# A two-layer hybrid encoder on one core: the last layer's residual in two exact parts, two tiles' statistics on ScalarE, and the order of two matmuls in the mean square

## The chip, the cores and the metric

The kernel runs on one core of one Trainium2 chip. The metric is the device time of the whole kernel in microseconds (us): the median over runs. A core has TensorE (PE in the profile, with its weight loads shown as PEld), VectorE (DVE), ScalarE (ACT), GpSimd (POOL) and SyncE (SP, which only issues DMAs here). Each engine takes its own instructions strictly in the order in which they are written into its queue, and waits at an instruction until what it reads is there and what it overwrites is no longer needed.

## The reference, cut to what matters

Two layers on a 1024 x 1024 fp32 input. Layer 0 has dilated attention and a gated linear attention (GLA), layer 1 a gated scan with 12 heads (HGRN2). Each layer ends in an output projection, a residual and a layer norm:

```python
def _layer_norm(z, g, b):
    mu = jnp.mean(z32, axis=-1, keepdims=True)
    var = jnp.mean(jnp.square(z32 - mu), axis=-1, keepdims=True)
    out = (z32 - mu) * lax.rsqrt(var + NORM_EPS) * g + b

def _head_rmsnorm(o, gain):
    o = o * lax.rsqrt(jnp.mean(o * o, axis=-1, keepdims=True) + NORM_EPS)
    return o.reshape(o.shape[0], o.shape[1], -1) * gain

# layer 1
q, f_f, f_b, i, gate = _split(proj, (C_WIDTH,) * 5)
o = bidirectional_gated_scan(qh, k_f, g_f, k_b, g_b, heads(i))
y = _head_rmsnorm(o, norm_gain) * jax.nn.silu(gate)
out = jnp.einsum('bsf,fd->bsd', y, w_out)
# every layer
x = _layer_norm(DEEPNORM_ALPHA * x + mixer(x), ln_gain[layer], ln_bias[layer])
```

## The kernel before, in words

**Exact parts.** The kernel keeps fp32 accuracy on TensorE by splitting an operand into a part rounded to fp32r (the H part, made by an ScalarE copy) and the exact rest (the L part, made by a subtraction on VectorE). A product is then three fp32r matmuls: H by H, L by H, H by L (`project`, lines 237 to 239; `out_units`; `final_units`, lines 321 to 323).

**Stages.** Attention runs first, then four GLA heads, then twelve HGRN heads. For every head 128 columns of the input projection are made in two halves of 512 tokens (hf 0 and 1) out of `xH[hf]` and `xL[hf]`, the transposed activations, which are 128 x 8 x 512 tiles that live through the layer. The head's scan has two directions d and two halves: `prep(d, hf)` makes decayed queries and keys, `keys` the states, `scores` the local products, `output(hf)` the head's result. The order within an HGRN head is (1,1), (1,0), (0,0), output(0), (0,1), output(1). In `prep`, VectorE scans the log gates (line 743), ScalarE takes exponentials (`gE`, `qi`, `ki`), GpSimd makes about ten small factors from `gE` (lines 763 to 781, from `eT` through `Gq`, `Gk`, `F3q`, `F3k` to `dec`), and VectorE multiplies them in (lines 756 to 799). The scores need `k2`, which needs `Gk`; the transposed keys need `k3`, which needs `F3k`. Before the gates of the last direction the head switches ScalarE's function table to the sigmoid and back (`sigmoids`); the second of the two sigmoids there needs the head's last projected block.

**Mean square.** `output` squares the head's result, splits the square into `sqH` (ScalarE, line 902) and `sqL` (VectorE, line 904), and sums it over partitions with two matmuls against a tile of ones, `sqH` first (lines 905 and 906). There are 8 such sums in the GLA stage and 24 in the HGRN stage.

**The end of the last layer.** Heads 10 and 11 leave their output projection to `final_units`. For each of the eight token tiles, `pre` puts the residual `z[i]` into two PSUM banks by an fp32 matmul against the identity (line 312), and `mul` adds twelve fp32r matmuls (lines 321 to 323). Tiles 4 to 7 are hf 1; tiles 4 and 6 use the two `pj` banks, tiles 5 and 7 the `s` and `o` banks, so tile 6 waits until tile 4 has been normalized. `layer_norm` takes the statistics on VectorE (line 374), and then, for tiles 0 to 5, normalizes on ScalarE (line 391), multiplies the gain on VectorE (line 392) and adds the bias on GpSimd (line 393); tiles 6 and 7 do all of that on VectorE (lines 382 and 384). The result goes out by DMA.

**Order.** A tile scheduler fixes each engine's order when the kernel is built, from the program's order, priorities and its own idea of when operands are ready. Work under `high_priority` is placed as if it stood 3000 instructions earlier.

Of the kernel before, what the change touches and what calls it, by code (L numbers as in the profile page):

```python
# [7 lines left out]
F32 = mybir.dt.float32  # L8
F32R = mybir.dt.float32r
U32 = mybir.dt.uint32  # L10
AF = mybir.ActivationFunctionType
ALU = mybir.AluOpType
# [3 lines left out]
P = 128  # L16
D = 1024
# [110 lines left out]
class Trunk:  # L128
# [156 lines left out]
    def final_units(self, w, f0, ys, norm, banks, reload):  # L285
# [7 lines left out]
        def weights(key):  # L293
# [12 lines left out]
                held[key] = first, res  # L306
            return held[key]

        def pre(hf, t):
            ps = [self.ps.tile([P, HALF], F32, tag=tag, name="fin", bufs=2) for tag in banks[hf][t % 2]]  # L310
            for c in range(2):
                mm(ps[c], self.ident, self.z[hf * 4 + t][:, c * HALF:(c + 1) * HALF], start=True, stop=False)
            tiles[hf, t] = ps

        def mul(hf, t):
            ts = slice(t * P, (t + 1) * P)
# [47 lines left out]
                res.append(t)  # L364
        return res

    def layer_norm(self, pool, i, params, direct=False, src=None):

        nc = self.nc
        zs = [self.z[i][:, c * HALF:(c + 1) * HALF] for c in range(2)]  # L370
        src = src or zs
        st = pool.tile([P, 2, 6], F32, tag="gt", name="st", bufs=2)
        for c in range(2):
            nc.vector.bn_stats(st[:, c, :], src[c])
        mv = pool.tile([P, 4], F32, tag="eT", name="mv", bufs=2)
        nc.vector.bn_aggr(mv[:, 0:2], st)
        mu, r, b = (mv[:, k:k + 1] for k in (0, 2, 3))
        self.act(r, mv[:, 1:2], AF.Ln, bias=self.epsz)
        self.act(r, r, AF.Exp, scale=-0.5)
        if direct:  # L380
            for c in range(2):
                nc.vector.scalar_tensor_tensor(zs[c], src[c], mu, params[c], op0=ALU.subtract, op1=ALU.mult)
            for c in range(2):
                nc.vector.scalar_tensor_tensor(zs[c], zs[c], r, params[2 + c], op0=ALU.mult, op1=ALU.add)
            return
        nc.vector.scalar_tensor_tensor(b, mu, -1.0, r, op0=ALU.mult, op1=ALU.mult)
        if src is zs:
            nc.scalar.activation(self.z[i], self.z[i], AF.Identity, scale=r, bias=b)
        for c in range(2):
            if src is not zs:  # L390
                nc.scalar.activation(zs[c], src[c], AF.Identity, scale=r, bias=b)
            nc.vector.tensor_tensor(zs[c], zs[c], params[c], op=ALU.mult)
            nc.gpsimd.tensor_tensor(zs[c], zs[c], params[2 + c], op=ALU.add)
# [300 lines left out]
class ScanHead(Item):  # L694
# [181 lines left out]
    def output(self, hf):  # L876
# [25 lines left out]
        nc.scalar.copy(sH, sq[0])  # L902
        sL = pool.tile([P, HALF], F32R, tag="k3", name="sqL", bufs=self.nbuf)
        nc.vector.tensor_tensor(sL, sq[0], sH.bitcast(F32), op=ALU.subtract)
        mm(ms, T.ones, sH, start=True, stop=False)
        mm(ms, T.ones, sL, start=False, stop=True)
        rs = pool.tile([P, HALF], F32, tag="tmp", name="rs", bufs=2)
        T.act(rs, ms, AF.Ln, scale=1.0 / self.V, bias=T.eps)
        T.act(rs, rs, AF.Exp, scale=-0.5)
# [222 lines left out]
def trunk_kernel(tc, x, x_t, w_in_ab, gla_gate_up, gla_gate_bias, gla_norm, w_out_ab, w_in_c, hgrn_lower_bounds,  # L1132
                 hgrn_norm, w_out_c, rel_bias, ln_gain, ln_bias, onehot, ident, mask, out):
    nc = tc.nc
    with ExitStack() as ctx:
# [14 lines left out]
        def scan_consts(pool):  # L1150

            T.restart = pool.tile([P, HALF], mybir.dt.uint8, tag="restart", name="restart")
            nc.gpsimd.memset(T.restart, 1)
            nc.gpsimd.memset(T.restart.rearrange("p (n c) -> p n c", c=16)[:, :, 0:1], 0)
            T.mask = pool.tile([P, P], U32, tag="mask", name="mask")
            nc.gpsimd.dma_start(T.mask, mask)
            T.ones = pool.tile([P, P], F32R, tag="ones", name="ones")
            nc.scalar.copy(T.ones, T.one.broadcast_to([P, P]))

# [90 lines left out]
        def ln1(i, halves):  # L1250
            if 1 not in lnp:
                lnp[1] = T.ln_params(hp, (("E", 5), ("E", 5)), ln_gain[1:2, :], ln_bias[1:2, :])
            T.layer_norm(hp, i, lnp[1], i in DIRECT[1], halves)
            if i in DIRECT[1]:
                for c in range(2):
                    nc.sync.dma_start(outv[:, i, c * HALF:(c + 1) * HALF], T.z[i][:, c * HALF:(c + 1) * HALF])
# [113 lines left out]
```

## Time and profile before

| what | value |
|---|---|
| time, median of 3 runs | 1990.66 us (1989.68 to 1991.99) |
| time of the profiled execution | 1991.2 us |
| its span (first to last instruction) | 1989.4 us |
| TensorE busy | 1914.5 us, 96% of the span |
| VectorE, ScalarE, GpSimd busy | 1320.6, 1010.1, 334.1 us |
| TensorE's mean granted clock | 0.992 of full speed |

The profile is of one execution; its time stands 0.5 us above the median. A span shown as x4 or x8 in the trace is a run of equal instructions. One fp32 matmul shows as two records of TensorE.

### The profile page before, as it was taken

What the parts mean: (1) busy time and instruction counts of PE and PEld (TensorE: products, weight loads), DVE (VectorE), ACT (ScalarE), POOL (GpSimd) and SP (SyncE); (2) the same over time, 40 slices, a digit from 0 to 9 for tenths busy, and PEclk for the clock granted to TensorE, in tenths of its full rate; (3) what the DMA queues carried; (4) which work ended last, traced back from release to release, by engine and by line L of the source; (5) the groups of instructions that cost most, each with busy time, mean ns of one, the idle gap of its engine ahead of it and who ended that gap; (6) DMA issues with size and microseconds to landing.
All of it is one profiled execution on the core that took longest, in us unless ns stands there. A gap on an engine that the chain in (4) does not pass through costs nothing.

```text
span 1989.4 us, 35447 instructions
## 1 busy us (share of the span) xinstructions
PE 1914.5 (96%) x13887; PEld 1571.8 (79%) x13887; DVE 1320.6 (66%) x2761; ACT 1010.1 (51%) x1847; POOL 334.1 (17%) x848
## 2 busy tenths in 40 slices
PE   7999999999999999999999999999999999999997
PEld 4777777787787878867878888888888888888875
DVE  4697878774776675677767646655764664676478
ACT  4666656553544343444556445535544642654473
POOL 1110202001211111111123112111311111131124
PEclk8999999999999999999999999999999999999999
DMA  8321212123111212112411211121121112112112
GB/s 234 71 50 33 50 38 45 31 77 95 43 50 50 64 53 70 53 43 69 124 43 43 64 54 44 38 80 33 33 79 49 33 48 71 32 39 89 40 44 85
DMA packets 142866, 118.59 MB, mean 60 GB/s; under 512 B 15301, under 2 KB 122565, under 8 KB 142699
## 3 DMA queue, kind: packets, MB, share of 16 engines
q1 hardware_dynamic: 130027, 102.55, 17.6%
q0 software_dynamic: 4512, 11.47, 2.4%
q10 hardware_dynamic: 8160, 2.31, 0.6%
q8 instruction: 109, 1.79, 0.4%
q14 instruction: 58, 0.48, 0.1%
HBM read 108.19 MB, written 8.11 MB: 58 GB/s over the span
## 4 chain that ended last, share of the span: by engine, by line
PE 46%; DVE 8%; ACT 4%; DMA 3%; issue 2%; POOL 1%; DVEq 0%; ACTq 0%; POOLq 0%
PE pj L237 9%; PE pj L238 9%; PE pj L239 9%; PE kv L818 3%; DVE g L743 2%; PE po L271 2%; PE po L272 2%; PE s L844 2%; PE po L273 2%; PE pj L249 1%; PE pj L250 1%; PE pj L251 1%; DMA wraw<-in_w_in_c_dram 1%; PE o L888 1%; PE o L892 1%
## 5 line engine op out<-in xcount | busy, mean ns | idle before, releaser
L237 PE MATMUL pj<-xH,wH 128*128 128x512 f32 x1280 | 512.7, 401 | 2.8 <-DVE kl L531 1.3
L238 PE MATMUL pj<-xL,wH 128*128 128x512 f32 x1280 | 508.1, 397 | 0.0
L239 PE MATMUL pj<-xH,wL 128*128 128x512 f32 x1280 | 507.4, 396 | 0.0
L199 ACT CAST wH<-wraw 128x512 fp32r<-128x512 f32 x248 | 153.5, 619 | 294.3 <-PE pj L238 180.3
L200 DVE TENSOR_TENSOR wL<-wraw,wH 128x512 fp32r<-128x512 f32 x248 | 170.8, 689 | 195.2 <-ACT wH L199 182.8
L237 PEld LDWEIGHTS pj<-xH,wH 128*128 128x128 f32 x1280 | 242.0, 189 | 51.1 <-issue 2.0
L239 PEld LDWEIGHTS pj<-xH,wL 128*128 128x128 f32 x1280 | 241.9, 189 | 46.3 <-issue 0.2
L238 PEld LDWEIGHTS pj<-xL,wH 128*128 128x128 f32 x1280 | 242.1, 189 | 44.2
L763 POOL TENSOR_TENSOR eT<-gE 128x16 f32<-128x16 f32 x64 | 30.2, 472 | 1038.2 <-ACT gE L158 1038.2
L249 PE MATMUL pj<-wH,xH 128*128 128x256 f32 x640 | 182.1, 285 | 0.4 <-ACT v L726 0.3
L250 PE MATMUL pj<-wL,xH 128*128 128x256 f32 x640 | 180.8, 283 | 0.0
L251 PE MATMUL pj<-wH,xL 128*128 128x256 f32 x640 | 180.7, 283 | 0.0
L276 DVE TENSOR_TENSOR z<-z,po 128x512 f32<-128x512 f32 x200 | 134.9, 682 | 63.5 <-PE po L273 62.7
L271 PE MATMUL po<-woH,yH 128*128 128x512 f32 x336 | 138.3, 421 | 9.7 <-ACT woH L217 6.3
L272 PE MATMUL po<-woL,yH 128*128 128x512 f32 x336 | 134.7, 401 | 0.7 <-DVE woL L218 0.6
L273 PE MATMUL po<-woH,yL 128*128 128x512 f32 x336 | 132.2, 394 | 0.0
L249 PEld LDWEIGHTS pj<-wH,xH 128*128 128x128 f32 x640 | 122.0, 191 | 4.3 <-ACT v L726 1.0
L250 PEld LDWEIGHTS pj<-wL,xH 128*128 128x128 f32 x640 | 122.1, 191 | 2.9
L251 PEld LDWEIGHTS pj<-wH,xL 128*128 128x128 f32 x640 | 122.0, 191 | 2.7
L271 PEld LDWEIGHTS po<-woH,yH 128*128 128x128 f32 x336 | 62.0, 188 | 33.9 <-ACT woH L217 10.9
L818 PE MATMUL kv<-v,k3T 128*128 128x128 f32 (+1 forms) x448 | 80.0, 313 | 7.9 <-DVE stb L830 5.2
L217 ACT CAST woH<-wraw 128x512 fp32r<-128x512 f32 x80 | 47.5, 616 | 76.9 <-PE po L273 26.7
(230 smaller groups left out, 3841.0 us busy)
## 6 DMA issues: line engine op xcount, KB each, us to landing
wraw<-in_w_in_c_dram SPq DMA_DIRECT2D x152, 256.0 KB
wraw<-in_w_in_ab_dram SPq DMA_DIRECT2D x96, 256.0 KB
wraw<-in_w_out_c_dram SPq DMA_DIRECT2D x44, 256.0 KB
wraw<-in_w_out_ab_dram SPq DMA_DIRECT2D x40, 256.0 KB
z<-in_x_dram SPq DMA_DIRECT2D x8, 512.0 KB
strip<-line POOLq DMA_DIRECT2D x8, 448.0 KB, 5.8
park<-sp SPq DMA_DIRECT2D x14, 256.0 KB
out_dram<-z SPq DMA_DIRECT2D x6, 512.0 KB
```

Source lines behind the costliest of these rows:

```text
L199: self.nc.scalar.copy(h, raw)
L200: self.nc.vector.tensor_tensor(lo, raw, h.bitcast(F32), op=ALU.subtract)
L237: mm(ps[:m], wH, xH[:, k, :], start=(k == 0), stop=False)
L238: mm(ps[:m], wH, xL[:, k, :], start=False, stop=False)
L239: self.lastmm = mm(ps[:m], wL, xH[:, k, :], start=False, stop=(k == last)).ins
L249: self.nc.tensor.matmul(o, xH, wH, start=(k == 0 and i % 2 == 0), stop=False)
L250: self.nc.tensor.matmul(o, xH, wL, start=False, stop=False)
L251: self.lastmm = self.nc.tensor.matmul(o, xL, wH, start=False, stop=(k == KT - 1 and i % 2 == 1)).ins
L271: mm(ps, yH[:, ts], h, start=(b == 0), stop=False)
L272: mm(ps, yH[:, ts], lo, start=False, stop=False)
L273: mm(ps, yL[:, ts], h, start=False, stop=(b == nb - 1))
L818: nc.tensor.matmul(kv[:, j, :], k3T[:, t, :], self.val(hf * 4 + t), start=True, stop=True)
```

## The change

1. In the last layer, for hf 1, the residual of tiles 4 to 7 is split ahead: ScalarE copies `z[4+t]` into two of the eight columns of `xH[0]` (rounded to fp32r), GpSimd subtracts that from `z` into `xL[0]`. Both tiles are dead once the last head's hf 0 projection has read them. `pre` then uses two fp32r matmuls against `identr`, an fp32r identity that ScalarE makes at the start of each of the two later stages, in place of one fp32 matmul. hf 0 keeps the fp32 matmuls.
2. Tiles 4 and 5 of the last layer take their statistics on ScalarE: a copy with a running sum and a square with a running sum for each 512 columns, with three one-column operations on VectorE between them, in place of two `bn_stats` and one `bn_aggr`.
3. In every mean square `sqL` enters the sum first and `sqH` second.

```diff
+        def split(t):
+            z = self.z[4 + t]
+            zH, zL = (x[0][:, 2 * t:2 * t + 2, :].rearrange("p a c -> p (a c)") for x in (self.xH, self.xL))
+            with self.tc.high_priority(offset=3000):
+                self.nc.scalar.copy(zH, z)
+                self.nc.gpsimd.tensor_tensor(zL, z, zH.bitcast(F32), op=ALU.subtract)
+
         def pre(hf, t):
             ps = [self.ps.tile([P, HALF], F32, tag=tag, name="fin", bufs=2) for tag in banks[hf][t % 2]]
+            tiles[hf, t] = ps
+            if hf == 1 and not reload:
+                if t == 0:
+                    for k in range(4):
+                        split(k)
+                for c in range(2):
+                    mm(ps[c], self.identr, self.xH[0][:, 2 * t + c, :], start=True, stop=False)
+                    mm(ps[c], self.identr, self.xL[0][:, 2 * t + c, :], start=False, stop=False)
+                return
             for c in range(2):
                 mm(ps[c], self.ident, self.z[hf * 4 + t][:, c * HALF:(c + 1) * HALF], start=True, stop=False)
...
+        if by_act:
+            sums = st.rearrange("p a b -> p (a b)")
+            for c in range(2):
+                nc.scalar.activation(zs[c], src[c], AF.Copy, accum_out=sums[:, c:c + 1])
+            nc.vector.tensor_scalar(sums[:, 2:3], sums[:, 0:1], sums[:, 1:2], -1.0 / D, op0=ALU.add, op1=ALU.mult)
+            for c in range(2):
+                nc.scalar.activation(zs[c], src[c], AF.Square, bias=sums[:, 2:3], accum_out=sums[:, 3 + c:4 + c])
+            nc.vector.tensor_scalar(mv[:, 1:2], sums[:, 3:4], sums[:, 4:5], 1.0 / D, op0=ALU.add, op1=ALU.mult)
+            nc.vector.tensor_scalar(mu, sums[:, 2:3], -1.0, None, op0=ALU.mult)
+        else:
+            for c in range(2):
+                nc.vector.bn_stats(st[:, c, :], src[c])
+            nc.vector.bn_aggr(mv[:, 0:2], st)
...
-        mm(ms, T.ones, sH, start=True, stop=False)
-        mm(ms, T.ones, sL, start=False, stop=True)
+        mm(ms, T.ones, sL, start=True, stop=False)
+        mm(ms, T.ones, sH, start=False, stop=True)
```

The diff does not say where the new instructions land. Three places of the order do; line numbers are those of the kernel that the rows are from.

GpSimd in the last head, from the end of the (1,1) factors on. Before, the (1,0) factors follow at once:

```order
L781 TENSOR_TENSOR dec_20313<-PP_20305 128x4
L763 TENSOR_TENSOR eT_20392<-gE_20383 128x16
L769 COPY Gq_20394<-gE_20383 128x8
L771 COPY Gk_20395<-gE_20383 128x8
L768 TENSOR_TENSOR Gq_20394<-gE_20383,eT_20392 128x8
L770 TENSOR_TENSOR Gk_20395<-gE_20383,eT_20392 128x8
L773 TENSOR_TENSOR PP_20400<-eT_20392 128x8
L776 COPY F3q_20402<-Gq_20394 128x4x2
L778 COPY F3k_20403<-Gk_20395 128x4x2
```

The same place in the change (`xL_69` is `xL[0]`, `z_75` to `z_78` are the residuals of tiles 4 to 7):

```order
L807 TENSOR_TENSOR dec_20317<-PP_20309 128x4
L315 TENSOR_TENSOR xL_69<-z_75,xH_67 128x1024
L315 TENSOR_TENSOR xL_69<-z_76,xH_67 128x1024
L789 TENSOR_TENSOR eT_20396<-gE_20387 128x16
L795 COPY Gq_20398<-gE_20387 128x8
L797 COPY Gk_20399<-gE_20387 128x8
L379 DMA lnp_20806<-in_ln_gain_dram 128x512
L315 TENSOR_TENSOR xL_69<-z_77,xH_67 128x1024
L794 TENSOR_TENSOR Gq_20398<-gE_20387,eT_20396 128x8
L796 TENSOR_TENSOR Gk_20399<-gE_20387,eT_20396 128x8
```

Two subtractions stand ahead of the (1,0) factors and a third in their middle, ahead of `Gk`; the fourth follows a second load of norm parameters, just ahead of the (0,0) factors.

ScalarE in the last head, where (1,1) and (1,0) get their exponentials. Before:

```order
L158 ACTIVATE gE_20288<-gt_20286 128x32
L217 CAST woH_20626<-wraw_20632 128x512
L158 ACTIVATE qi_20291<-g_20283 128x512
L712 ACTIVATE F_20270<-pj_20245 128x512
L158 ACTIVATE ki_20292<-g_20283 128x512
L158 ACTIVATE gE_20383<-gt_20381 128x32
L158 ACTIVATE qi_20386<-g_20378 128x512
L158 ACTIVATE ki_20387<-g_20378 128x512
L1109 ACT_TABLE_LOAD
```

And in the change:

```order
L217 CAST woH_20630<-wraw_20636 128x512
L738 ACTIVATE F_20274<-pj_20249 128x512
L158 ACTIVATE gE_20292<-gt_20290 128x32
L158 ACTIVATE qi_20295<-g_20287 128x512
L314 CAST xH_67<-z_75 128x1024
L158 ACTIVATE ki_20296<-g_20287 128x512
L314 CAST xH_67<-z_76 128x1024
L158 ACTIVATE gE_20387<-gt_20385 128x32
L314 CAST xH_67<-z_77 128x1024
L158 ACTIVATE qi_20390<-g_20382 128x512
L158 ACTIVATE ki_20391<-g_20382 128x512
```

Three of the four copies stand between these exponentials. Further down, the log gate of (0,0), line 158, moves from ahead of the copies of the (1,0) scores to behind them, and `gE`, `qi` and `ki` of (0,0) and one weight cast move from ahead of the copy of the last projected block to behind it, directly ahead of the switch to the sigmoid; the copy of the (0,0) keys moves behind the switch back.

ScalarE in the tail. Before, tiles 4 and 5 need it for the two roots and the normalizing passes:

```order
L158 ACTIVATE mv_20965<-mv_20965,sc_89 128x1
L158 ACTIVATE mv_20965<-mv_20965 128x1
L391 ACTIVATE z_75<-fin_20942,mv_20965 128x512
L391 ACTIVATE z_75<-fin_20943,mv_20965 128x512
L158 ACTIVATE mv_20996<-mv_20996,sc_89 128x1
L158 ACTIVATE mv_20996<-mv_20996 128x1
L391 ACTIVATE z_76<-fin_20946,mv_20996 128x512
```

In the change (`fin_20946` and `fin_20947` are tile 4, `fin_20960` and `fin_20961` tile 5):

```order
L394 ACTIVATE z_75,st_20978<-fin_20946 128x512
L394 ACTIVATE z_75,st_20978<-fin_20947 128x512
L394 ACTIVATE z_76,st_21015<-fin_20960 128x512
L397 ACTIVATE z_75,st_20978<-fin_20946,st_20978 128x512
L397 ACTIVATE z_75,st_20978<-fin_20947,st_20978 128x512
L394 ACTIVATE z_76,st_21015<-fin_20961 128x512
L158 ACTIVATE mv_20979<-mv_20979,sc_89 128x1
L158 ACTIVATE mv_20979<-mv_20979 128x1
L397 ACTIVATE z_76,st_21015<-fin_20960,st_21015 128x512
L417 ACTIVATE z_75<-fin_20946,mv_20979 128x512
L417 ACTIVATE z_75<-fin_20947,mv_20979 128x512
```

Four passes over each tile are new, and those of tile 5 stand among those of tile 4.

On TensorE, before, the last head's last but one projected block (24 matmuls) is broken off after 15 for the transposed keys and the scores of (1,1). In the change 23 of its matmuls come first. Behind the (1,1) scores stand 9 of the last block's 24 matmuls, then the (1,0) scores, 9 more, the (1,1) states and the (1,0) keys, and its last 6; before, 19 of the 24 stood behind the (1,0) states. In the tail the twelve matmuls of tile 7 but two stand ahead of tile 6, and those two are the last of the kernel. The mean square's pair stands, in most heads, where `sqL` stood before; in 6 of the 24 HGRN sums it stands three matmuls later. SyncE's order is unchanged.

## Rows read from the trace of the kernel before

**Rows 1.** The page, part 1: busy time, share of the span, instructions.

```profile
PE 1914.5 (96%) x13887; PEld 1571.8 (79%) x13887; DVE 1320.6 (66%) x2761; ACT 1010.1 (51%) x1847; POOL 334.1 (17%) x848
```

**Rows 2.** Windows: length, busy of each engine, TensorE's clock, DMA share, GB/s.

```profile
872.00:876.00 4.00, 1.52 (x4) 0.37 (x2) 1.39 (x2) 1.86 (x4) 0.00 (x0) 1.00 0.17 50
876.00:880.00 4.00, 3.22 (x5) 1.13 (x5) 3.14 (x6) 3.28 (x6) 0.00 (x0) 0.55 0.00 0
880.00:884.00 4.00, 4.00 (x12) 2.77 (x11) 2.48 (x4) 0.24 (x2) 1.07 (x8) 0.59 0.01 4
```

**Rows 3.** Timeline of TensorE, one mean square: start, length, what.

```profile
1886.11 0.40 PE L238 MATMUL pj<-xL,wH 128*128 128x512 f32 x1
1886.45 0.49 PE L905 MATMUL tr<-sqH,ones 128*128 128x512 f32 x1
1886.78 0.39 PE L239 MATMUL pj<-xH,wL 128*128 128x512 f32 x1
1887.01 0.40 PE L237 MATMUL pj<-xH,wH 128*128 128x512 f32 x1
1887.25 0.43 PE L906 MATMUL tr<-sqL,ones 128*128 128x512 f32 x1
```

**Rows 4.** Waits of the weight loads: us in total, times, longest.

```profile
PEld tr L905 <- ACT sqH L902: 12.3, 27, 2.0
PEld tr L906 <- DVE sqL L904: 6.6, 24, 1.5
```

**Rows 5.** Timeline of GpSimd, last head (idle before it in brackets).

```profile
1915.82 0.66 POOL L763 TENSOR_TENSOR eT<-gE 128x16 f32<-128x16 f32 x1
...
1919.56 0.20 POOL L779 TENSOR_TENSOR F3k<-Gk,PP 128x8 f32<-128x8 f32 x1
...
1919.86 0.58 POOL L363 DMA_DIRECT2D lnp<-in_ln_gain_dram  x1
...
1924.70 0.33 POOL L763 TENSOR_TENSOR eT<-gE 128x16 f32<-128x16 f32 x1 [3.73 <-ACT gE L158]
```

**Rows 6.** GpSimd's bias additions, line 393: shortest/median/longest in ns, starts, form.

```profile
L393 POOL TENSOR_TENSOR z<-z,lnp x20: 1260/1661/1734, 892.3 to 1978.5; 128x512 f32<-128x512 f32 x20
```

**Rows 7.** Timeline of GpSimd in the tail.

```profile
1952.87 3.41 POOL L393 TENSOR_TENSOR z<-z,lnp 128x512 f32<-128x512 f32 x2 [11.11 <-DVE z L392]
```

**Rows 8.** Timeline of VectorE in the tail.

```profile
1953.37 1.76 DVE L904 TENSOR_TENSOR sqL<-tmp,sqH 128x512 fp32r<-128x512 f32 x1
...
1984.64 1.41 DVE L384 SCALAR_TENSOR_TENSOR z<-z,mv,lnp 128x512 f32<-128x512 f32 x2
```

**Rows 9.** Timeline of TensorE, last head and tail.

```profile
1916.46 0.66 PE L809 MATMUL tr<-ident,k 128*128 128x128 f32 x4 [1.18 <-DVE k L787]
...
1921.55 0.25 PE L844 MATMUL s<-q,k 128*32 128x64 f32 x2
...
1930.97 0.40 PE L239 MATMUL pj<-xH,wL 128*128 128x512 f32 x1
...
1964.26 1.98 PE L312 MATMUL fin<-z,ident 128*128 128x512 f32 x4 [0.28 <-ACT z L391]
```

**Rows 10.** Timeline of ScalarE, last head.

```profile
1910.66 0.23 ACT L158 ACTIVATE gE<-gt 128x32 f32<-128x32 f32 x1 [0.36 <-DVE gt L746]
...
1931.41 0.60 ACT L712 ACTIVATE F<-pj 128x512 f32<-128x512 f32 x1 [1.72 <-PE pj L239]
...
1935.78 0.81 ACT L158 ACTIVATE g<-F,lb,oml 128x512 f32<-128x512 f32 x1
```

**Rows 11.** ScalarE's line 1236: lengths in ns as in rows 6.

```profile
L1236 ACT CAST xH<-z x8: 1031/1044/1051, 6.0 to 32.3; 128x1024 fp32r<-128x1024 f32 x8
```

**Rows 12.** ScalarE's line 158: the read-out of a running sum.

```profile
L158 ACT ACTIVATION_READ_ACCUMULATOR p<-p,m x64: 181/187/202, 65.8 to 426.8; 128x1 f32 x64
```

**Rows 13.** Instructions on the tile `fin`: VectorE's statistics, ScalarE's normalizing pass.

```profile
L374 DVE BATCH_NORM_STATS2 st<-fin x24: 644/686/700, 884.2 to 1982.4; 128x6 f32<-128x512 f32 x24
L391 ACT ACTIVATE z<-fin,mv x20: 769/776/782, 890.7 to 1975.7; 128x512 f32<-128x512 f32 x20
```

More of the change, by code (lines that the diff above doesn't have):

```diff
@@ L307, in weights @@
             return held[key]
+        def split(t):
[4 more added lines that the diff above has]
+                self.nc.gpsimd.tensor_tensor(zL, z, zH.bitcast(F32), op=ALU.subtract)
         def pre(hf, t):
             ps = [self.ps.tile([P, HALF], F32, tag=tag, name="fin", bufs=2) for tag in banks[hf][t % 2]]
+            tiles[hf, t] = ps
[7 more added lines that the diff above has]
+                return
             for c in range(2):
                 mm(ps[c], self.ident, self.z[hf * 4 + t][:, c * HALF:(c + 1) * HALF], start=True, stop=False)
-            tiles[hf, t] = ps
         def mul(hf, t):
@@ L365, in ln_params, with layer_norm @@
         return res
-    def layer_norm(self, pool, i, params, direct=False, src=None):
+    def layer_norm(self, pool, i, params, direct=False, src=None, by_act=False):
         nc = self.nc
@@ L372, in layer_norm @@
         st = pool.tile([P, 2, 6], F32, tag="gt", name="st", bufs=2)
-        for c in range(2):
-            nc.vector.bn_stats(st[:, c, :], src[c])
         mv = pool.tile([P, 4], F32, tag="eT", name="mv", bufs=2)
-        nc.vector.bn_aggr(mv[:, 0:2], st)
         mu, r, b = (mv[:, k:k + 1] for k in (0, 2, 3))
+        if by_act:
[11 more added lines that the diff above has]
+            nc.vector.bn_aggr(mv[:, 0:2], st)
         self.act(r, mv[:, 1:2], AF.Ln, bias=self.epsz)
@@ L1156, in scan_consts @@
             nc.gpsimd.dma_start(T.mask, mask)
+            T.identr = pool.tile([P, P], F32R, tag="identr", name="identr")
+            nc.scalar.copy(T.identr, T.ident)
             T.ones = pool.tile([P, P], F32R, tag="ones", name="ones")
@@ L1252, in ln1 @@
                 lnp[1] = T.ln_params(hp, (("E", 5), ("E", 5)), ln_gain[1:2, :], ln_bias[1:2, :])
-            T.layer_norm(hp, i, lnp[1], i in DIRECT[1], halves)
+            T.layer_norm(hp, i, lnp[1], i in DIRECT[1], halves, i in (4, 5))
             if i in DIRECT[1]:
```

## The prediction, made before the change was run

> **What bounds the kernel now.** The page's first part comes first: TensorE is busy for 96% of the span and no other engine for more than 66% [rows 1]. So what shortens TensorE's queue counts nearly everywhere, and what lets TensorE wait counts too. The windows come next, because the average hides two places: where a layer ends, TensorE waits, and after a window in which it was busy for 1.52 of 4 us its granted clock averaged 0.55 and 0.59 of full speed over the next 8 us [rows 2], so it ran mostly at the lower of its two levels (1.2 of 2.4 GHz). Then the timelines of the last head (from 1910 us) and of the tail. There TensorE holds back a stock of projection matmuls that fill its time while the chain of the head's scan runs over ScalarE, GpSimd and VectorE: its one wait at the first transposed keys is 1.18 us, the (1,0) scores start at 1921.55, the last projected block ends at 1931.4 [rows 9], ScalarE copies it, switches to the sigmoid and back and starts the (0,1) gates at 1935.78 [rows 10]. From there the head's last output, four normalizations and the tail follow. In the tail TensorE is released at 1964.26 by ScalarE's pass over tile 2 [rows 9], and VectorE ends the work at 1984.64 + 1.41 = 1986.05 [rows 8].
>
> The sum is made against the profiled execution's 1991.2 us, which is 0.5 us above the median of 1990.66. From no change this kernel's measurement can tell about 0.2%, 4 us: within that means 1986.7 to 1994.6.
>
> **The mean square.** Before, TensorE reaches `sqH` a little early: 0.34 us after the matmul ahead and 0.33 us before the next, where plain neighbours stand 0.23 apart (1886.78 to 1887.01). That is 0.21 us lost; `sqL` costs 0.24 after its forerunner, 0.01 lost [rows 3]. The weight loads waited for `sqH` 27 times and for `sqL` 24 times [rows 4]. If every such loss at `sqH` went and nothing came for it, 24 x 0.21 = 5 us would be saved: the upper end. But the pair now stands where `sqL` stood, TensorE gets there 0.2 us sooner because it no longer paused, and `sqL` comes no earlier: the wait changes its operand. Only the 6 sums that stand three matmuls later escape it, 6 x 0.21 = 1.3 us. The sum closes one matmul (0.23) later. I take -1; ends -5 and +1.
>
> **The subtractions on GpSimd.** No row shows one of 1024 columns. Two of 512 columns bound it: 2 x 1.26 = 2.5 to 2 x 1.73 = 3.5 us [rows 6]. I take 3.0, as GpSimd will run beside a busy VectorE. For a 2048-column addition the Trainium skill (GPSIMD Engine Reference, Elementwise — side-by-side cycle accounting) gives 4497 ns; halved, an estimate of 2.25 us, and with it the sum below would end at 1998. The rows here, doubled, are longer than that, and they price the sum.
>
> They also shut out VectorE. While GpSimd made two additions from 1952.87 [rows 7], a VectorE subtraction took 1.76 us [rows 8], about 1.1 us longer than a VectorE pass of that width without GpSimd beside it (two in 1.41 us [rows 8]). So the time on GpSimd isn't hidden behind VectorE.
>
> Before, the (1,0) factors begin at 1915.82, right behind the (1,1) factors, and their `F3k` ends at 1919.56 + 0.20 = 1919.76, 3.9 us later [rows 5]. Now three subtractions and one load of 0.58 us stand in that stretch: 3 x 3.0 + 0.6 = 9.6 us later (8.1 to 11.1). ScalarE's own delay lies beside it: three copies of 1.04 [rows 11], 3.1 us, end before GpSimd has done its second subtraction. The multiplications and the (1,0) scores follow as before, so the scores slide from 1921.55 to about 1931.2.
>
> **What that moves.** Before, 1931.4 - 1921.55 = 9.8 us pass between the start of these scores and the end of the last projected block [rows 9]. Now 15 projection matmuls stand behind the scores, 15 x 0.23 = 3.5 us; with the scores, states and keys there I put 5.5 us. So 9.8 - 5.5 = 4.3 us of the delay are made up, because TensorE did its projections earlier; 9.6 - 4.3 = 5.3 us are left, and the last block ends near 1936.7. ScalarE then needs 1935.78 - 1931.41 = 4.4 us to the (0,1) gates as before [rows 10], plus what has moved in between: `gE` 0.23 [rows 10], one weight cast, `qi`, `ki` and the key copy at about 0.5 start to start, 2.2 us together. The (0,1) gates come 5.3 + 2.2 = 7.5 us late (6.0 to 9.0). The rest of the head hangs on them, and VectorE still has the (0,0) states and masks to make there: +8 in all. If the fourth subtraction also falls between VectorE's products for the (1,0) scores, 3 more.
>
> **The clock.** TensorE has nothing but the scores to run while it waits for them, some 5 us or more. The windows show what followed such a pause [rows 2]. The 15 matmuls behind it at half speed would cost 3.5 us more. Ends 0 and 3.5; I take +1.5, since the pause's place against the clock's changes is open.
>
> **The tail.** An fp32 residual matmul takes 1.98 / 2 = 0.99 us at most [rows 9], two fp32r ones 0.46. Eight are replaced: about 4 us less TensorE, of which six stand behind 1964.26, 2.8 to 3.2 us. But three things eat it. A ScalarE pass with a sum costs 0.6 (as the copy out of PSUM at 1931.41 [rows 10]) and 0.19 to read it out [rows 12], 0.8. From TensorE's release R, tile 4 is through at R + 16 x 0.23 = 3.7; ScalarE then needs about seven such passes (three of tile 5 stand among them), the roots and a pass of 0.78 [rows 13] before the first bank is free: R + 9.7. TensorE, 39 matmuls on, is there at R + 9.0 and waits 0.7 us. It ends at R + 13.9; before, tile 6 alone ended at R + 13.9 (36 x 0.23 and six fp32 matmuls), so tile 6 gains 0.5 us. Last, tile 7 now ends with tile 6, not alone after it, and VectorE's two gain products for tile 5 stand ahead of tile 6's second statistics and wait for ScalarE's late pass (R + 13.1). Then VectorE has three statistics of 0.69 [rows 13] and eight passes of 0.70 (1.41 for two [rows 8]), 7.7 us: it ends near R + 22.2 (two products of 0.7 from R + 13.1, then these), against 1986.05 - 1964.26 = R + 21.8 before. I take +0.4; ends -2 (the passes cost less and nothing waits) and +1.5. The two casts of the identity are done while TensorE has work; the parts for hf 1 are due before that stage.
>
> **Sum:** 1991.2 - 1 + 8 + 1.5 + 0.4 = 2000.1; I predict **2000.0 us**, slower. Its own bounds, a few ends at a time: 1994 to 2004.
>
> **Rivals.**
> - *The subtractions are covered* (not slower). GpSimd was idle for 3.73 us before the (0,0) factors [rows 5] and TensorE has its projections early, so the delay could vanish in the 4.3 us that are made up. That decides itself at one price: 3p + 0.6 below 4.3, a subtraction of 1.2 us, under half of the lowest bound. Or the gates of (0,1) have slack that I don't see. Then only the mean square and the tail are left: 1991.2 - 1.5 - 1 = 1988.5; with both at their better ends, 1991.2 - 5 - 2 = 1984. Against it: in-order queues, and the factors stand behind the subtractions.
> - *The mean square pays in full.* If `sqL` is always there when TensorE comes, -5 in place of -1: 1996. For it: in some heads `sqL` was not waited for at all. Against it: 24 waits at `sqL` [rows 4].
> - *Everything collides.* VectorE and GpSimd take turns, one long subtraction for each short VectorE operation, the fourth subtraction falls between the (1,0) products (+3), and the lower clock lasts over both waits, at the (1,1) and the (1,0) scores (+2 over what I took): 2005.
>
> **How the numbers follow.** Forecast 0.52, covered 0.20, full pay 0.10, collision 0.18. Of the covered case I put 0.11 below 1986.7 and 0.09 within; of the forecast 0.08 falls below 1994.6. So faster 0.11, same 0.17, slower 0.72. A tenth below and a tenth above are left out of the range: 1988 to 2006.
>
> **What would show it.** In the profile after: four GpSimd subtractions of 2.5 to 3.5 us between about 1916 and 1935; the (1,0) `F3k` near 1929; TensorE idle for some microseconds ahead of the (1,0) scores, with a window of lower clock behind; the (0,1) gates near 1943; the tail from the release of the `pj` banks to VectorE's end about 22 us as before. I am wrong if the subtractions take near 1.2 us, if the last projected block still ends near 1931, or if the tail shrinks by 2 us or more.

## The result, and the profile after

The change makes the kernel slower: 2005.74 us median of five runs (2003.93 to 2007.73) against 1990.66 (1987.75 to 1991.99). The ratio is 1.0076, with a 95% interval of 1.0065 to 1.0087: 15.1 us between the medians. The profiled execution of after is the fastest of its five (2003.93 us, span 2002.1, granted clock 0.988), so between the two profiles only 12.7 us are to be found (span before 1989.4).

The place is the last head, as the windows of after show (columns as in [rows 2]; the head begins at 1905.17):

```profile
1912.00:1916.00 4.00, 2.19 (x10) 1.50 (x8) 3.35 (x6) 3.98 (x8) 4.00 (x10) 1.00 0.23 66
1916.00:1920.00 4.00, 1.54 (x5) 1.03 (x5) 4.00 (x3) 3.96 (x5) 4.00 (x4) 0.54 0.00 0
1920.00:1924.00 4.00, 3.62 (x68) 3.28 (x69) 4.00 (x4) 2.50 (x5) 3.98 (x6) 0.50 0.25 72
1924.00:1928.00 4.00, 2.44 (x6) 1.34 (x5) 3.01 (x3) 0.00 (x0) 3.98 (x10) 0.68 0.26 59
1928.00:1932.00 4.00, 2.72 (x68) 2.39 (x69) 1.74 (x4) 1.32 (x3) 0.17 (x1) 0.75 0.04 10
1932.00:1936.00 4.00, 4.00 (x22) 3.44 (x21) 0.80 (x3) 0.99 (x3) 0.00 (x0) 0.82 0.00 0
```

GpSimd is busy from end to end for 16 us. VectorE is counted as busy nearly throughout, but has only 6, 3, 4 and 3 instructions in the first four windows. TensorE waits, and its granted clock falls to 0.50, its lower level of 1.2 GHz. The timeline of VectorE in after says why VectorE completes so little, and what it waits for next:

```profile
1914.82 2.65 DVE L813 TENSOR_TENSOR k<-ki,F3k 128x512 f32<-128x512 f32 x1
1917.39 2.57 DVE L819 TENSOR_TENSOR k<-ki,gE 128x256 f32<-128x256 f32 x1
...
1921.45 2.73 DVE L818 TENSOR_TENSOR q<-qi,gE 128x256 f32<-128x256 f32 x1
...
1925.78 2.69 DVE L819 TENSOR_TENSOR k<-ki,gE 128x256 f32<-128x256 f32 x1
...
1935.13 0.29 DVE L854 COPY stb<-kv 128x128 f32<-128x128 f32 x1 [5.39 <-PE kv L844]
...
1946.79 1.21 DVE L769 TENSOR_TENSOR_SCAN g<-restart,g 128x512 f32<-128x512 uint8 x1
```

Elsewhere the first of these four products takes 0.68 us and the others 0.41 to 0.42. Each ran beside one of the four subtractions and ended 0.3 to 0.6 us behind it. GpSimd's timeline in after:

```profile
1914.13 5.55 POOL L315 TENSOR_TENSOR xL<-z,xH 128x1024 fp32r<-128x1024 f32 x2
1919.65 0.39 POOL L789 TENSOR_TENSOR eT<-gE 128x16 f32<-128x16 f32 x1
...
1921.52 2.37 POOL L315 TENSOR_TENSOR xL<-z,xH 128x1024 fp32r<-128x1024 f32 x1
...
1925.82 2.35 POOL L315 TENSOR_TENSOR xL<-z,xH 128x1024 fp32r<-128x1024 f32 x1
```

TensorE's timeline in after holds the forecast's next stations: the wait at the first transposed keys (3.33 us, 1.18 in [rows 9]), the (1,0) scores, and behind them projection matmuls that start 0.43 us apart, where plain neighbours stood 0.23 apart in [rows 3]:

```profile
1917.53 1.11 PE L835 MATMUL tr<-ident,k 128*128 128x128 f32 x4 [3.33 <-DVE k L813]
...
1929.28 0.25 PE L870 MATMUL s<-q,k 128*32 128x64 f32 x2 [2.85 <-DVE k L824]
...
1931.55 0.63 PE L239 MATMUL pj<-xH,wL 128*128 128x512 f32 x1
1931.98 0.63 PE L237 MATMUL pj<-xH,wH 128*128 128x512 f32 x1
...
1976.97 0.50 PE L325 MATMUL fin<-xH,identr 128*128 128x512 f32 x1 [1.08 <-ACT z L417]
```

ScalarE's timeline in after answers to [rows 10], with two marks more: the first cast of the output weights, at which I let the last head begin, and the square of the last output (0,1), at which I let it end:

```profile
1905.17 0.61 ACT L217 CAST woH<-wraw 128x512 fp32r<-128x512 f32 x1
...
1936.85 0.60 ACT L738 ACTIVATE F<-pj 128x512 f32<-128x512 f32 x1 [0.39 <-PE pj L239]
...
1944.05 0.81 ACT L158 ACTIVATE g<-F,lb,oml 128x512 f32<-128x512 f32 x1
...
1964.61 0.59 ACT L924 ACTIVATE tmp<-o 128x512 f32<-128x512 f32 x1
```

The same two marks in the timeline of ScalarE before:

```profile
1907.24 0.61 ACT L217 CAST woH<-wraw 128x512 fp32r<-128x512 f32 x1
...
1950.80 0.60 ACT L898 ACTIVATE tmp<-o 128x512 f32<-128x512 f32 x1 [0.16 <-PE o L890]
```

VectorE's timeline in after ends with these two passes:

```profile
1997.30 1.40 DVE L410 SCALAR_TENSOR_TENSOR z<-z,mv,lnp 128x512 f32<-128x512 f32 x2
```

With VectorE's end (after 1997.30 + 1.40 = 1998.70; before 1986.05 [rows 8]) these marks cut each program in three, and all that follows is read against them:

| | until the last head | last head | tail | sum |
|---|---|---|---|---|
| before | 1907.24 | 43.56 | 35.25 | 1986.05 |
| after | 1905.17 | 59.44 | 34.09 | 1998.70 |
| difference | -2.07 | +15.88 | -1.16 | +12.65 |

The first column can't be credited to the change. Kernels below with the same mean square entered the last head anywhere from 1901.8 to 1909.6 in their profiled executions, and one with the old one at 1906.54. The 15.88 is far outside that, and the last head's own length repeats well: it is 42.72 to 42.74 in the four kernels below that leave the subtractions out of it.

### The profile page after: what moved, and what is told of

It reads as the page before. It is cut to its first block, busy times and chain, and to the rows that moved or that the text cites. A ratio compares the mean times of both kernels' runs of the same rounds, so it can differ in the third digit from the quotient of the medians.

```text
span 2002.1 us, 35435 instructions
## 1 busy us (share of the span) xinstructions
PE 1914.3 (96%) x13887; PEld 1577.1 (79%) x13887; DVE 1324.8 (66%) x2761; ACT 1017.6 (51%) x1869; POOL 337.6 (17%) x852
## 3 DMA queue, kind: packets, MB, share of 16 engines
q10 hardware_dynamic: 8160, 2.31, 0.5%
## 5 line engine op out<-in xcount | busy, mean ns | idle before, releaser
L271 PE MATMUL po<-woH,yH 128*128 128x512 f32 x336 | 139.0, 422 | 10.3 <-ACT woH L217 6.6
```

The lines of the kernel that those rows point to most:

```text
L271: mm(ps, yH[:, ts], h, start=(b == 0), stop=False)
```

## The experiments

All ran with the kernel before on the same chip. Beside the time of each, the marks of its profiled execution are used. Two questions were open. Is it the split alone that costs? And does it cost through its place in GpSimd's queue, through VectorE's waiting, or through the clock?

### The split taken away

```diff
-            if hf == 1 and not reload:
+            if False:
```

> The changed kernel with the residual of the last four tiles entered as fp32 again, as before; the new order of the mean square and the statistics on ScalarE stay. Theory (the parts made on GpSimd cost everything, about 15 us against the changed kernel): the last head runs as before, the (1,0) scores start near 1920, the (0,1) gates near 1934; about 2 us are gained by the order of the mean square, the tail grows by 0 to 2 us since eight fp32 matmuls are back; 1987 to 1991 us, at least 13 us below the changed kernel. Rival (the other two edits carry a part of the loss, for instance the ScalarE statistics in the tail): above 1994 us.

Measured: 1992.88 us median against 1990.31, ratio 1.0015 (1.0006 to 1.0024). That is 12.9 us below the changed kernel, and between the two ranges, 1.9 us above the theory's. The last head takes 42.74 us, slightly less than before. So the split is what makes the last head long. But the kernel isn't faster than before either, and a small loss is left: in the profile (of a long execution, 1995.2 us) the tail takes 37.95 us, 2.7 more than before. The next kernel is this one without ScalarE's statistics; its head is as long and its tail takes 36.36. So by the profiles these statistics cost 1.6 us while the residual enters as fp32. By the times it is open, since the two intervals overlap.

### The mean square alone

The kernel before with the two matmuls exchanged. (The fp32r identity is made too, and not used.)

```diff
-        mm(ms, T.ones, sH, start=True, stop=False)
-        mm(ms, T.ones, sL, start=False, stop=True)
+        mm(ms, T.ones, sL, start=True, stop=False)
+        mm(ms, T.ones, sH, start=False, stop=True)
```

> The kernel before with the new order of the mean square (sqL first) and nothing else. Theory (the wait changes its operand): within 2 us of the kernel before, 1988.5 to 1991.5 us; the weight loads wait for sqL in place of sqH about as often. Rival (it pays in full): 1984 to 1987 us. Second rival (the scheduler's other order costs, as the 2.6 us that the changed kernel without the split lost against before): 1992 to 1995 us.

Measured: 1990.73 us against 1989.77, ratio 1.0004 (0.9995 to 1.0013). It makes no difference that can be told: at best 1 us less, at worst 2.6 more. In its profile the last head takes 42.72 us, 0.8 less than before, and the tail 36.36, 1.1 more; the order of the mean square alone moves that much between the two columns. What became of the 24 x 0.21 us is seen in TensorE's timeline in after, one mean square:

```profile
1883.98 0.39 PE L238 MATMUL pj<-xL,wH 128*128 128x512 f32 x1
1884.46 0.47 PE L931 MATMUL tr<-sqL,ones 128*128 128x512 f32 x1
1884.77 0.40 PE L932 MATMUL tr<-sqH,ones 128*128 128x512 f32 x1
1885.00 0.39 PE L239 MATMUL pj<-xH,wL 128*128 128x512 f32 x1
```

The pair starts 0.48 us behind its forerunner, 0.25 more than plain neighbours, and another 0.08 are lost inside it. Before, it lost 0.22 [rows 3]. Over all 32 such pairs the medians say the same: 0.44 and 0.31 in after, which is 0.29 lost in a pair, and before 0.34 and 0.34 about `sqH`, 0.24 and 0.25 about `sqL`, which is 0.25. The waits of the weight loads in after, as in [rows 4], add that the wait for the operand itself is gone but for one:

```profile
PEld tr L931 <- PE pj L238: 6.8, 14, 0.5
...
PEld tr L931 <- DVE sqL L930: 2.8, 1, 2.8
```

So the waits on which the rival rests have gone, as it said they might, and the theory's "about as often" is wrong. But TensorE still pauses ahead of the pair, now behind a matmul, and no time is gained. Why it pauses there is open.

### The subtractions behind the (1,0) factors

The changed kernel with the old order of the mean square. No line of the split is touched, but the order of the program then comes out another way: GpSimd gets all four subtractions behind the (1,0) factors, where in after two stand ahead of these factors, one among them and one behind.

```diff
-        mm(ms, T.ones, sL, start=True, stop=False)
-        mm(ms, T.ones, sH, start=False, stop=True)
+        mm(ms, T.ones, sH, start=True, stop=False)
+        mm(ms, T.ones, sL, start=False, stop=True)
```

> The changed kernel with sqH first in the mean square again. The order of the program then also puts all four GpSimd subtractions behind the (1,0) factors and ahead of the (0,0) factors. Theory A (what counts is that the subtractions stand ahead of the (1,0) factors on GpSimd's queue): the (1,0) F3k ends near 1920 and its scores start near 1922, TensorE's clock stays up, the last projected block ends near 1931, and only the (0,0) factors come late, by 4.7 us (four subtractions of 2.4 after 1919.8, against 1924.7); 1991 to 1996 us. Theory B (the shut-out of VectorE counts wherever the subtractions stand): VectorE still loses 4 x 2 us in a stretch in which it is busy; 1998 to 2006 us.

Measured: 2007.28 us, ratio 1.0083 (1.0070 to 1.0097): as slow as the change. Theory A falls. B's mechanism holds; the time is 1.3 us above its range, since VectorE loses 9.4 us here and not 8. The factors come early (`eT` at 1915.12, 8.6 us behind the mark, as before), and still the (1,0) scores start at 1930.35, 23.8 us behind it. VectorE's timeline in this run:

```profile
1919.71 2.71 DVE L819 TENSOR_TENSOR k<-ki,gE 128x256 f32<-128x256 f32 x1
1922.34 7.53 DVE L823 TENSOR_TENSOR q<-qi,Gq 128x256 f32<-128x256 f32 x1
...
1936.75 0.29 DVE L854 COPY stb<-kv 128x128 f32<-128x128 f32 x1 [5.95 <-PE kv L844]
```

and GpSimd's, beside it:

```profile
1919.76 2.37 POOL L315 TENSOR_TENSOR xL<-z,xH 128x1024 fp32r<-128x1024 f32 x1
...
1922.65 6.93 POOL L315 TENSOR_TENSOR xL<-z,xH 128x1024 fp32r<-128x1024 f32 x3
```

One product of 0.41 us lasted 7.53 us: VectorE was let in only when three subtractions, back to back, were done (1922.65 + 6.93 = 1929.58). By the Trainium skill (SBUF — State Buffer, Who interferes with whom) the engine that comes second is blocked until the other's instruction is finished. The trace agrees in part. The four products of after each ended just behind one subtraction. But this one waited for three, and by the rows it began 0.31 us ahead of the first of them; two of the four began 0.04 and 0.07 us ahead of theirs. So the rows don't show who came second.

### The subtractions on VectorE

```diff
-                self.nc.gpsimd.tensor_tensor(zL, z, zH.bitcast(F32), op=ALU.subtract)
+                self.nc.vector.tensor_tensor(zL, z, zH.bitcast(F32), op=ALU.subtract)
```

> The changed kernel with the four subtractions on VectorE in place of GpSimd, 1.4 us each by two passes of 0.7, 5.5 us in all, ahead of the (1,1) and (1,0) products. GpSimd's queue is as before, and nothing is locked. Theory (the price is what stands ahead of the (1,0) scores, less the 4 us that TensorE makes up): the (1,0) scores start about 5 us later than before, the last projected block 1 to 3 us later; 1992 to 1998 us. Rival (any work of this kind in that stretch costs the whole 15 us): 2002 us or more. Second rival (VectorE has room there): 1988 to 1990 us.

Measured: 1993.85 us against 1990.31, ratio 1.0019 (1.0010 to 1.0028). On the engine that was thought too busy, the same work costs a quarter of what it costs on the idle one. Here VectorE's timeline has each of them at 1.22 us, half of GpSimd's 2.35:

```profile
1913.57 1.22 DVE L315 TENSOR_TENSOR xL<-z,xH 128x1024 fp32r<-128x1024 f32 x1
...
1918.53 1.23 DVE L315 TENSOR_TENSOR xL<-z,xH 128x1024 fp32r<-128x1024 f32 x1
```

All four are 4.8 us of added work on VectorE, and the last head takes 47.84 us, 4.3 more than before. So VectorE has hardly any slack in this head: what it is given appears nearly in full. It appears although the other path is not late. The (1,0) scores start 4.4 us later than before, as expected, but the last projected block is copied 3.8 us sooner, and not 1 to 3 us later. So the (0,1) gates start 27.8 us behind this run's mark of 1906.24, before 28.5; the scan behind them waits for VectorE. ScalarE's and VectorE's timelines in this run:

```profile
1934.05 0.82 ACT L158 ACTIVATE g<-F,lb,oml 128x512 f32<-128x512 f32 x1
...
1936.29 1.22 DVE L769 TENSOR_TENSOR_SCAN g<-restart,g 128x512 f32<-128x512 uint8 x1
```

Before, VectorE had waited for these gates (its timeline there):

```profile
1936.63 1.23 DVE L743 TENSOR_TENSOR_SCAN g<-restart,g 128x512 f32<-128x512 uint8 x1 [1.24 <-ACT g L158]
```

### The subtractions later

The split without its raised priority; the subtractions then stand between the (0,0) and the (0,1) factors.

```diff
-            with self.tc.high_priority(offset=3000):
-                self.nc.scalar.copy(zH, z)
-                self.nc.gpsimd.tensor_tensor(zL, z, zH.bitcast(F32), op=ALU.subtract)
+            self.nc.scalar.copy(zH, z)
+            self.nc.gpsimd.tensor_tensor(zL, z, zH.bitcast(F32), op=ALU.subtract)
```

> The changed kernel without the raised priority of the split. The four subtractions then stand between the (0,0) and the (0,1) factors on GpSimd, where it idled from 1927 to 1937 in the kernel before; the casts stand later on ScalarE, the last one behind the (0,1) gates. Theory A (position ahead of the (1,0) factors is the cause): the first part of the last head is as before, (1,0) scores near 1920, the fourth cast is late, so the (0,1) factors come some 3 us late; 1989 to 1995 us. Theory B (the shut-out of VectorE): VectorE's short operations ahead of the (0,1) scan take 2.4 us each, four of them, up to 8 us; 1996 to 2003 us.

Measured: 1996.78 us against 1990.31, ratio 1.0030 (1.0019 to 1.0042). More than half of the loss is gone, but the place where GpSimd had idled for 10 us isn't free: a VectorE product of 0.68 us lasted 5.03 beside two subtractions there, one of 0.68 lasted 2.79, and the scan of 1.21 lasted 1.89; 7.1 us in all. The longest of them in VectorE's timeline of this run, and GpSimd's subtractions beside it:

```profile
1929.73 5.03 DVE L812 TENSOR_TENSOR k<-ki,F3k 128x512 f32<-128x512 f32 x1
...
1929.56 4.65 POOL L314 TENSOR_TENSOR xL<-z,xH 128x1024 fp32r<-128x1024 f32 x2
```

The last head takes 51.09 us, 7.5 more than before. The time lies at the lower end of B's range, and the trace shows B's mechanism.

### The subtractions in pieces

```diff
-                self.nc.gpsimd.tensor_tensor(zL, z, zH.bitcast(F32), op=ALU.subtract)
+                for q in range(8):
+                    qs = slice(q * P, (q + 1) * P)
+                    self.nc.gpsimd.tensor_tensor(zL[:, qs], z[:, qs], zH[:, qs].bitcast(F32), op=ALU.subtract)
```

> The changed kernel with each of the four GpSimd subtractions cut into eight of 128 columns, at the same places of GpSimd's queue. Theory A (VectorE waits for one GpSimd instruction at a time, so the length of one is what hurts): a product on VectorE waits some 0.3 to 0.6 us and not 2.4, the (1,0) scores start 4 us or more sooner than in the changed kernel, and the time is 1994 to 2000 us. Theory B (VectorE waits until GpSimd has no such instruction ready any more, as where one product lasted 7.53 us beside three subtractions): nothing is gained, 2003 to 2010 us.

Measured: 2008.82 us, ratio 1.0099 (1.0085 to 1.0113). The time lies in B's range, but neither theory has the mechanism quite. Most products ran almost freely (0.68 us where 0.41 is usual). But eight pieces cost GpSimd 3.32 us while VectorE waits, against 2.35 in one, and the first eight, beside VectorE's products, 5.73. So now GpSimd's queue is what is late, and VectorE waits for the (1,0) factors; its timeline:

```profile
1928.12 0.69 DVE L815 TENSOR_TENSOR k<-ki,F3k 128x512 f32<-128x512 f32 x1 [9.45 <-POOL F3k L807]
1928.72 3.65 DVE L821 TENSOR_TENSOR k<-ki,gE 128x256 f32<-128x256 f32 x1
...
1939.78 0.29 DVE L856 COPY stb<-kv 128x128 f32<-128x128 f32 x1 [6.13 <-PE kv L846]
```

The second of these rows waited for a run of eight pieces (1928.77 + 3.32 = 1932.09). Why VectorE gets in between pieces at one time and not at another is left open.

### The (0,0) scan taken ahead

In after, the (0,0) scan starts 30.9 us behind the mark. It stands on ScalarE behind copies of the (1,0) scores and on VectorE behind the state copy that waits 5.39 us. This run lifts the gates and the scan over both; the subtractions stay.

```diff
+        with ExitStack() as st:
+            if (d, hf) == (0, 0) and getattr(self, "apart", False):
+                st.enter_context(T.tc.high_priority(offset=300))
-        g = self.gate_log(d, hf)
+            g = self.gate_log(d, hf)
...
-        nc.vector.tensor_tensor_scan(run, T.restart, run, 0.0, op0=M, op1=ALU.add)
+            nc.vector.tensor_tensor_scan(run, T.restart, run, 0.0, op0=M, op1=ALU.add)
```

> The changed kernel with the (0,0) gates and their scan raised in priority: ScalarE then makes the gates ahead of the (1,0) score copies (it waited 7.32 us there, before 1930.65), and VectorE scans them ahead of the first state copy of (1,1) (it waited 5.39 us there, before 1935.13). The four subtractions stay where they were. Theory (the late (1,0) scores hurt through the (0,0) scan, which stood behind these two waits and started 13.9 us later than before, and not through the last projected block, 5.4 us late): the (0,0) factors start near 1932 in place of 1938, the (0,1) scan starts 3 to 5 us sooner, 1999 to 2002.5 us. Rival (the last projected block and the table switches behind it hold the (0,1) gates as before): 2004 to 2008 us.

Measured: 2005.65 us, ratio 1.0079 (1.0065 to 1.0092). The theory falls. VectorE's timeline in this run:

```profile
1931.16 1.21 DVE L772 TENSOR_TENSOR_SCAN g<-restart,g 128x512 f32<-128x512 uint8 x1
...
1937.32 0.29 DVE L857 COPY stb<-kv 128x128 f32<-128x128 f32 x1 [4.26 <-PE kv L847]
...
1948.45 1.22 DVE L772 TENSOR_TENSOR_SCAN g<-restart,g 128x512 f32<-128x512 uint8 x1
```

The (0,0) scan is 6.4 us sooner (24.5 behind this run's mark of 1906.66), and the wait stands behind it. The (0,1) scan is where it was: 41.8 us behind the mark, 41.6 in after. Between the two rows VectorE idles for 0.31 us only. So it isn't this scan's place that counts. VectorE stands still until TensorE's states for (1,1) are there, and then has the states, products and masks of (0,0) to do, one behind the other. The rival's gates are late too: those of (0,1) start 38.3 us behind the mark, in after 38.9. But they end 2.7 us before the scan begins, so it is VectorE that holds it.

### TensorE kept busy

Eight matmuls are added behind the (1,1) scores; the scores of (1,0) overwrite what they write.

```diff
+        if (d, hf) == (1, 0) and getattr(self, "apart", False):
+            for n in range(8):
+                mm(X.rearrange("p a c -> p (a c)"), T.ones, T.xH[1][:, 0, :], start=True, stop=True)
```

> The changed kernel with eight added matmuls of 512 columns (ones times a part of x, overwritten by the scores) on TensorE between the (1,1) and the (1,0) scores. They leave nothing out. Theory (the lower clock costs little, since TensorE waits for products anyway): the matmuls behind the (1,0) scores stand 0.23 apart in place of 0.43, the last projected block ends 0 to 1.5 us sooner, and the time is 2003 to 2007 us. Rival (the lower clock is a large part of the 15 us): 2001 us or less. Second rival (the added matmuls themselves run at half speed, 8 x 0.43 = 3.4 us, and end behind the wait): 2007 to 2009 us.

Measured: 2004.09 us, ratio 1.0068 (1.0055 to 1.0081), against 1.0078 and 1.0079 for the two other runs on the same chip. The time is in the theory's range, but the run didn't take the lower clock away. The eight matmuls ran at the lower level themselves (3.66 us for eight), and the (1,0) scores behind them too. TensorE is back at 0.23 from matmul to matmul 3.3 us behind the start of these scores (1929.84 to 1933.12), in after 4.3 us (1929.28 to 1933.57); the first matmul for the states comes 4.7 us behind that start and 4.8 in after. The wait at the state copy is 5.21 us and not 5.39. So what the clock costs as a whole stays open. In after's rows the seven projections at the lower level behind the scores take 3.0 us from start to start, where 0.23 each would be 1.6: 1.4 us are lost on this path.

### The statistics on VectorE again

The changed kernel with `by_act` left at False.

```diff
-            T.layer_norm(hp, i, lnp[1], i in DIRECT[1], halves, i in (4, 5))
+            T.layer_norm(hp, i, lnp[1], i in DIRECT[1], halves)
```

> The changed kernel with the statistics of all tiles on VectorE again; the four subtractions stand at the same places of GpSimd's queue. Theory (the last head is all, ScalarE's statistics are worth a microsecond either way in the tail): VectorE's end comes 33 to 36 us behind the last output (34.1 in the changed kernel, 35.3 before), 2004 to 2008 us. Rival (with the cheaper residual and without ScalarE's statistics the tail shrinks by 3 us): 2001 to 2003 us.

Measured: 2005.78 us, ratio 1.0078 (1.0065 to 1.0091): no difference to the change that can be told, within some 3 us. The profiled execution is the longest of the five (2010.47); in it the tail takes 35.36 us, in after 34.09, and the last head 60.26. So by the tails of the profiles ScalarE's statistics gain 1.3 us with the split, where they cost 1.6 without it.

### Two tiles split, in the tail

Only tiles 6 and 7 are split, the rest by VectorE behind the gain products of tile 3, once with ScalarE's statistics and once without.

```diff
-            if hf == 1 and not reload:
-                if t == 0:
-                    for k in range(4):
-                        split(k)
+            if hf == 1 and not reload and t >= 2:
+                split(t)
...
+            with self.tc.issue_after(self.lastnorm):
+                self.nc.vector.tensor_tensor(zL, z, zH.bitcast(F32), op=ALU.subtract)
```

> The changed kernel with the split for tiles 6 and 7 alone, the rest by VectorE behind the gain products of tile 3, where VectorE waits for others; tiles 4 and 5 enter as fp32. Theory (the place is what costs; in the tail VectorE has room, and TensorE saves 4 x 0.5 us ahead of the last tiles): the last head is as before, the tail from the last output 1 to 3 us shorter than without any split; 1989 to 1992 us. Rival (VectorE's late subtractions hold up the statistics of tiles 4 and 5): 1993 to 1996 us.

> The same two late splits, with the statistics of all tiles on VectorE as before. Theory: TensorE ends 2 us sooner, but VectorE also has the statistics of tiles 4 and 5 and two subtractions of 1.2 us there and becomes the end; 1988 to 1991 us, within 2 us of the kernel before. Rival (ScalarE's statistics were the loss in the tail without the split): 1986 to 1988 us.

Measured: 1995.77 us with ScalarE's statistics, ratio 1.0029 (1.0018 to 1.0041), and 1993.22 without, 1.0023 (1.0013 to 1.0033). The last head is as without any split (42.73 us in both), but the tail takes 39.94 and 39.23 us. In the first of them the two subtractions on VectorE lasted 2.31 and 2.16 us, where 1.22 is their length, beside GpSimd's bias additions, and one-column operations of the statistics stand behind both. Its theory falls, its rival holds. The second run, whose profiled execution is the fastest of nine (1989.97), misses theory and rival: it is slower than either said, and one of its subtractions lasted 1.90 us. No version here beats the kernel before.

## Why the prediction was right in direction and short in size

The forecast was 2000.0 us, within 1988 to 2006 and slower; it came out 5.7 us longer, near the rival in which everything collides (2005). The result lies 0.3 us inside the range and 1.7 us above the forecast's own bounds (1994 to 2004). That the range holds it is partly luck. Times below are counted from the mark at which the last head begins.

**Confirmed: the (1,0) scores.** They were to slide by 9.65 us; they slid from 14.31 [rows 9] to 24.11, 9.8 us. The sum was made up another way, though. The subtractions took 2.35 to 2.80 us and not 3.0, and the factors among them 2.5 us in place of 3.9, so `F3k` ended 7.4 us later (12.52 before [rows 5], 19.96 in after) and not 9.6. The Trainium skill's figure (GPSIMD Engine Reference, Elementwise — side-by-side cycle accounting), halved, was an estimate of 2.25 us; the two that stood apart, at 2.37 and 2.35, lie between it and my lower bound of 2.5. The other two, 5.55 us together, are within my bounds. The rest came from the fourth subtraction, which did fall between VectorE's products (1925.78: 2.69 us for 0.42, so 2.3 us). I had priced that at 3 us and left it to a rival.

**Confirmed in kind: gates and lower clock.** The last projected block's copy came 7.5 us late (forecast 5.3), the (0,1) gates 10.3 (forecast 7.5). From the start of the (1,0) scores to the end of the last block it took 7.5 us and not 5.5, so 2.3 us were made up and not 4.3. The clock fell to 0.50 as foreseen and, by TensorE's rows, accounts for 1.4 of these 2 us, close to the 1.5 taken, though no run took the lower clock away. (Before, by TensorE's timeline, 16 and not 19 of the last block's matmuls stood behind the (1,0) states; the sum doesn't use it.)

**Failed: "The rest of the head hangs on them [...]: +8 in all."** With the clock the forecast had 9.5 us for this head; the last output came 15.9 us late. This is the term that was mis-sized. Up to the gates 1.3 of the 6.4 us are missing (10.3 for 7.5 and the clock's 1.5). The other 5.1 come behind the gates, where the forecast added 0.5 us and 5.6 came: the (0,1) scan starts 1.9 us behind the gates' end in after, 0.03 before, and from that scan to the last output it takes 17.8 us and not 14.2 (15.0 with the mean square alone). I let the delay run through TensorE and ScalarE and made no account of VectorE's queue, although I had written that GpSimd shuts it out and that VectorE still has (0,0) work there. The table takes VectorE's rows between the two marks: the length of a row beyond the shortest of its kind in the kernel before (counted where that is over 0.3 us), and the idle times in brackets beyond the 5.67 us of before.

| kernel | last head, over before | stretched rows | more idle | work added | sum |
|---|---|---|---|---|---|
| after | +15.9 | 8.7 | 7.1 | | 15.8 |
| behind the (1,0) factors | +15.0 | 9.4 | 4.3 | | 13.7 |
| on VectorE | +4.3 | | 0.0 | 4.8 | 4.8 |
| later | +7.5 | 7.1 | -0.2 | | 6.9 |
| in pieces | +20.9 | 3.2 | 16.2 | | 19.4 |
| scan ahead | +15.0 | 8.7 | 5.4 | | 14.1 |
| added matmuls | +14.5 | 8.7 | 5.5 | | 14.2 |
| statistics on VectorE | +16.7 | 8.7 | 8.0 | | 16.7 |
| no split | -0.8 | | 0.2 | | 0.2 |

That busy and idle time add up to the length is no finding. The finding is that nothing was taken up: the kernel before left VectorE 5.67 us of idle time in this head, and no run made up for more than 0.2 us of stretched rows or added work out of it. In after, VectorE first loses 8.7 us in four rows. Through them TensorE's (1,0) scores are late; behind the scores stand its projections, half of them at the lower clock, and the states of (1,1). VectorE waits 5.39 us for these at 1935.13, 30.0 us behind the mark. Its first state copy stood at 14.8 before, in VectorE's timeline there:

```profile
1922.01 0.28 DVE L828 COPY stb<-kv 128x128 f32<-128x128 f32 x1
```

From there its queue holds some 10 us of work ahead of the (0,1) scan. The run with the (0,0) scan taken ahead shows that this scan's place within that work doesn't matter. The run with the subtractions on VectorE shows the queue by itself: the gates come 0.7 us sooner than before, and the head is 4.3 us longer.

Two paths are late, though, and no run parts them in after. With the added matmuls the (0,1) scan starts 0.03 us behind the end of its gates, so there the path over TensorE and ScalarE holds it, as in the kernel before. That VectorE's queue accounts for the whole of the 5.1 us is argued from the rows and not shown.

**The mean square (-1).** Measured at no difference, and the interval includes -1. The reason given, that the wait changes its operand, isn't what the trace shows: the weight loads hardly wait for `sqL`, and yet TensorE pauses as long.

**The tail (+0.4).** From TensorE's release R to the end it is 21.7 us (1976.97 to 1998.70), before 21.8: near the forecast of 22.2. TensorE waited 0.28 us for the first bank (forecast 0.7) and ended at R + 13.9, as forecast. The pieces are less exact. 3.7 + 7 x 0.8 + 0.78 is 10.1 and not 9.7, even without the roots. The bank came free at R + 9.4 all the same, because a pass and its read-out overlap: rows of 0.60 and 0.21 us follow each other every 0.57 us, and those of 0.71 and 0.23 every 0.66. And the covered rival's sum is 1988.7 and not 1988.5.

**Which rival.** "Everything collides" named the turns of VectorE and GpSimd and the fourth subtraction, and both happened as it says. The lower clock too lasted over both waits (0.54 and 0.50 in the windows from 1916 to 1924, 0.75 and 0.82 behind 1928), but that it costs the 2 us more isn't shown. The total is close partly by chance, since it too lacked VectorE's wait for the states.

## What to carry to other kernels

An engine that idles isn't free if its work shuts out a busier one: ask whose time the work takes, not who has time. Where an engine has hardly any slack, add up its own lost time, stretched rows and new idle time, beside following the delay through an engine that has work in stock. And a window in which an engine is busy throughout with three short instructions shows a wait, not work.

## What was not expected of the hardware

A VectorE product of 0.41 us lasted 7.53 us beside three GpSimd subtractions in a row, and 5.03 us (for 0.68) beside two, so the turn doesn't always pass to VectorE between two instructions of GpSimd. Cutting 1024 columns into eight pieces made them cost GpSimd 3.32 us for 2.35. And the same subtraction took VectorE 1.22 us.
